# One core, a two-layer trunk in float32r: the SwiGLU's gate and up as seven block products for eight, the down projection in two passes

## The chip, the cores and the metric

The kernel runs on one core of a Trainium2 chip. The metric is device time in microseconds (us), from the first to the last instruction of the program with what lies around it; it is the median of three runs.

## The reference

The reference is a decoder trunk of two post-norm layers on 1024 tokens of 1024 features. Layer 0 mixes tokens by a convolution beside a spatial gate, layer 1 by an RWKV-7 recurrence. Behind each mixer stands a SwiGLU feed-forward with 2816 hidden channels, and it is these two feed-forwards that the change rewrites:

```python
D_MODEL, SEQ, DEPTH, FFN_HIDDEN = 1024, 1024, 2, 2816
ALPHA = (2.0 * DEPTH) ** 0.25

def swiglu_ffn(x, w_in, w_out):
    gate, up = jnp.split(x @ w_in, 2, axis=-1)
    return (jax.nn.silu(gate) * up) @ w_out

# every layer:  x <- LN(ALPHA * x + mixer(x));  x <- LN(ALPHA * x + swiglu_ffn(x))
```

## The kernel before

**Order of the program.** `phase_a` is the mixer of layer 0. `scan_const` builds the masks that the recurrence needs much later; it is some 85 operations on GpSimd. `ffn` follows for layer 0, then the projections and the scan of layer 1 (`phase_c`, `phase_d`), its output projection (`phase_e`), and `ffn` again. The order within each engine is made when the program is built: a scheduler places instructions by their dependencies, and each engine then runs its list in order.

**Dense products.** Each float32 operand is split into a head and a rest (`split`: ScalarE casts the head, VectorE subtracts it to get the rest; `load_unit` does this for a weight unit of 128x1024 at L185 and L186). A product is then three matmuls of 128x512 (head by head, head by rest, rest by head), written by `mm3` at L225 to L227.

**Norms ahead of the feed-forward.** `ln_to_T` norms a token tile of 128 tokens (`norm`, with a power on GpSimd at L265), transposes it on TensorE (`pt`, L284), applies gain and bias from PSUM into `lntmp` (VectorE and ScalarE in turn, L291 and L294), and splits it into eight pieces a layer half. `ln_rest` applies gain and bias to the token-major copy `acc` on GpSimd (L307, L308), one tile later; this copy is the residual.

**The feed-forward.** `up` makes one hidden tile of 128 channels: for each half of 512 tokens a gate product and an up product over eight feature tiles, so 2 x 2 x 8 x 3 = 96 matmuls, then silu, the product with the gate (`sg`, L578) and the split of the result (`hh`, `hl`). `down` takes hidden tiles in groups of two: for each token tile and each half of the output columns six matmuls into one PSUM bank, and VectorE adds the bank to `acc` (L595). The last group has four hidden tiles, and behind each token tile of it comes its final norm (`ln`, or `ln_out` for the output). There are 22 hidden tiles, so a feed-forward has 22 x 96 + 22 x 48 = 3168 matmuls. The first two hidden tiles begin with the first half of the tokens, while tiles of the second half are still being normed.

**Buffers.** Big tiles come from an arena of `N_ARENA` = 32 slots, raw loads from `N_RAW` = 3, weight units from `N_W` = 8, short-lived tiles from `N_T` = 6 and row broadcasts and masks (tag `row`) from 2.

Of the kernel before, what the change touches and what calls it, by code (L numbers as in the profile page):

```python
# [39 lines left out]
# columns: name -> number of [128] columns  # L40
# [44 lines left out]
def build(tc, xT, xtok, w_ab, w_abv, w_abo, cols, rows, hrows, sguw, f_in, f_out, w_r, w_k, w_v, w_o,  # L85
# [6 lines left out]
    with ExitStack() as es:  # L92
# [11 lines left out]
        xs, acc = phase_a(c, xT, xtok, w_ab, w_abv, w_abo, sguw, cols)  # L104
        show("a", acc)
        c.scan = scan_const(c)
        x1 = ffn(c, 0, xs, acc, f_in, f_out, "ffn0", fp32_out=True, spill=xres)
# [8 lines left out]
        xs, acc = phase_e(c, scry, xres, w_o, scan)  # L116
        if dbg is not None and "Y" in dbg:
            nc.sync.dma_start(dbg["Y"], scry)
        show("e", acc)
        ffn(c, 1, xs, acc, f_in, f_out, "ffn1", final=out)  # L120


# ---------------------------------------------------------------- helpers
# [52 lines left out]
def load_unit(c, src, arena=False, lo_eng=None):  # L176
    """A weight unit of [128, 1024]: raw load, then exact head / rest split."""
# [33 lines left out]
def act_half(c, name):  # L211
    """Split activations of 512 tokens, feature-major: 4 pieces of 2 feature tiles."""
# [8 lines left out]
def mm3(c, ps, lhs, rhs, start, stop, ls, rs):  # L221
    """ps += lhsT.T @ rhs with split operands; ls / rs slice them."""
# [7 lines left out]
def proj_T(c, ps, unit, xs, m=P):  # L230
    """ps[m, 512] = W[:, m columns].T @ x: feature-major output; unit is [128, 8 * m]."""
# [5 lines left out]
def proj_tok(c, ps, units, xs, t, turn=None):  # L237
    """ps[128 tokens, 512] = x.T @ W: token-major output; 4 units of [128, 2 * 512]."""
# [36 lines left out]
def ln_to_T(c, acc, tt, gname, g_row, b_row, dest, fp32_out=False, st=None, then=None):  # L275
    """LN of token tile acc (in place), and its transpose into dest (feature-major pieces)."""
# [3 lines left out]
    h, col = tt // 4, (tt % 4) * P  # L280
    for q in range(2):
# [3 lines left out]
        if not fp32_out:  # L285
            tm = tmp(c, "lntmp").rearrange("p (j t) -> p j t", j=4)
        for j in range(4):
            k = q * 4 + j
            d = dest[h][k // 2][:, k % 2, 1 + col:1 + col + P] if fp32_out else tm[:, j, :]
# [6 lines left out]
        if not fp32_out:  # L296
# [3 lines left out]
    c.rest = acc, g_row, b_row, then  # L300


def ln_rest(c):
    """Gain and bias of the token tile normed last: not needed soon, so behind the next one's norm."""
# [13 lines left out]
# ---------------------------------------------------------------- layer 0 mixer  # L318

def phase_a(c, xT, xtok, w_ab, w_abv, w_abo, sguw, cols):  # L320
# [15 lines left out]
    def load_consts():  # L336
# [6 lines left out]
        # keep s <= t: partition s, column t  # L343
# [7 lines left out]
    def pump(n=None):  # L351
        """A few steps of the convolution, to be done while the product traced last is."""
# [45 lines left out]
    def u_proj(j):  # L398
        """Feature tile j of the gated input, times the gate, and its split."""
# [15 lines left out]
    def v_proj(tt, units, v):  # L415
        """Token tile tt of the gate, up to its norm."""
# [118 lines left out]
    for tt in range(8):  # L535
# [9 lines left out]
        if tt % 4 == 3:  # L545
            xn[tt // 4] = act_half(c, "xm")
# [943 lines left out]
```

## Time and profile before

| what | value |
|---|---|
| runs of the kernel (us) | 2820.16, 2823.53, 2828.3; median 2823.53 |
| span of the profiled execution (us) | 2821.0 |
| TensorE busy, share of the span | 2686.7 us, 95% |
| VectorE busy | 1652.4 us, 59% |
| ScalarE busy | 1061.3 us, 38% |
| GpSimd busy | 753.0 us, 27% |
| mean granted TensorE clock | 0.974 |

The profile gives the span alone for the profiled execution; it stands 2.5 us under the median of the runs, and within their spread. PE is TensorE's matmuls, PEld its weight loads, DVE VectorE, ACT ScalarE, POOL GpSimd, SP the engine that issues most transfers. A row names line, engine, operation, and tiles as output<-inputs. `pu` and `pd` are the banks of the up and down products.

### The profile page before, as it was taken

Reading aid. Unit: us, or ns where it says so; the run is one execution under the profiler, and the core shown is the slowest. Engines: PE = TensorE matmul, PEld = TensorE weight load, DVE = VectorE, ACT = ScalarE, POOL = GpSimd, SP = SyncE. Lnnn points to the kernel's source line nnn. Section 1 sums busy time; section 2 is a strip of 40 time slices with the busy share of each in tenths; the row PEclk is TensorE's granted clock in tenths of the full one; section 3 lists DMA queues with packets and bytes.
Section 4 is the critical chain, followed back from the end, with each engine's and each line's share of the span. In section 5 each row is a group of like instructions: output and inputs, shape, how many; then the busy total and the mean of one; then the engine's idle time right before and its main releaser. Section 6 shows DMA issues by size and latency. Waiting matters only on the chain. (4 is left out here: it accounts for less than half of the span.)

```text
span 2821.0 us, 41373 instructions
## 1 busy us (share of the span) xinstructions
PE 2686.7 (95%) x16432; PEld 2180.9 (77%) x16432; DVE 1652.4 (59%) x2858; ACT 1061.3 (38%) x2060; POOL 753.0 (27%) x773
## 2 busy tenths in 40 slices
PE   8678999999999999799999999999989999999998
PEld 6466878888888887577777888888778888888887
DVE  7999673333333336878766899986663333333336
ACT  5435541111111113777655777775331111111111
POOL 4763472000000003210123777774340000000003
PEclk9889999999999999899998999999999999999999
DMA  4001302111111111445562222212211111111111
GB/s 162 30 15 46 112 31 74 45 45 48 57 45 45 47 51 49 153 135 183 153 212 96 71 83 67 68 54 91 101 53 53 45 45 57 48 45 45 53 45 60
DMA packets 119905, 205.98 MB, mean 73 GB/s; under 512 B 9888, under 2 KB 79648, under 8 KB 119712
## 3 DMA queue, kind: packets, MB, share of 16 engines
q1 hardware_dynamic: 117120, 196.01, 20.9%
q0 software_dynamic: 1440, 5.24, 0.5%
q8 instruction: 128, 2.10, 0.3%
q10 hardware_dynamic: 1152, 2.10, 0.2%
q14 instruction: 65, 0.53, 0.1%
HBM read 165.56 MB, written 37.75 MB: 72 GB/s over the span
## 5 line engine op out<-in xcount | busy, mean ns | idle before, releaser
L185 ACT CAST whi<-wraw 128x1024 fp32r<-128x1024 f32 x215 | 222.9, 1047 | 749.3 <-PE pd L226 355.7
L265 POOL TENSOR_TENSOR rstd<-ve,mhalf 128x1 f32<-128x1 f32 x48 | 40.6, 848 | 1470.3 <-DVE ve L263 1450.2
L186 DVE TENSOR_TENSOR wlo<-wraw,whi 128x1024 fp32r<-128x1024 f32 x215 | 271.5, 1271 | 244.5 <-ACT whi L185 216.5
L578 DVE TENSOR_TENSOR sg<-pu,sg 128x512 f32<-128x512 f32 x88 | 60.9, 692 | 500.8 <-PE pu L227 500.8
L595 DVE SCALAR_TENSOR_TENSOR acc<-acc,pd 128x512 f32<-128x512 f32 x320 | 218.2, 687 | 174.0 <-PE pd L227 173.9
L225 PE MATMUL pu<-xeh,whi 128*128 128x512 f32 x704 | 277.9, 395 | 0.0
L225 PE MATMUL pd<-whi,hh 128*128 128x512 f32 x704 | 277.3, 394 | 0.0
L227 PE MATMUL pd<-whi,hl 128*128 128x512 f32 x704 | 277.2, 394 | 0.0
L225 PE MATMUL pu<-xmh,whi 128*128 128x512 f32 x704 | 277.1, 394 | 0.0
L226 PE MATMUL pu<-xel,whi 128*128 128x512 f32 x704 | 276.8, 393 | 0.0
L226 PE MATMUL pu<-xml,whi 128*128 128x512 f32 x704 | 276.7, 393 | 0.0
L227 PE MATMUL pu<-xeh,wlo 128*128 128x512 f32 x704 | 276.7, 393 | 0.0
L226 PE MATMUL pd<-wlo,hh 128*128 128x512 f32 x704 | 276.7, 393 | 0.0
L227 PE MATMUL pu<-xmh,wlo 128*128 128x512 f32 x704 | 276.7, 393 | 0.0
L449 DVE SCALAR_TENSOR_TENSOR co<-yin,colt,co 128x512 f32<-128x512 f32 x150 | 167.3, 1126 | 1.7
L465 POOL TENSOR_TENSOR co<-ctap,co 128x512 f32<-128x512 f32 x90 | 144.1, 1602 | 51.0 <-ACT ctap L464 45.2
L227 PEld LDWEIGHTS pu<-xeh,wlo 128*128 128x128 f32 x704 | 132.3, 188 | 31.3
L226 PEld LDWEIGHTS pd<-wlo,hh 128*128 128x128 f32 x704 | 132.6, 188 | 30.7 <-DVE wlo L186 0.7
L225 PEld LDWEIGHTS pu<-xmh,whi 128*128 128x128 f32 x704 | 133.0, 189 | 30.0
L225 PEld LDWEIGHTS pu<-xeh,whi 128*128 128x128 f32 x704 | 132.7, 189 | 30.3
L226 PEld LDWEIGHTS pu<-xel,whi 128*128 128x128 f32 x704 | 132.5, 188 | 30.0
L225 PEld LDWEIGHTS pd<-whi,hh 128*128 128x128 f32 x704 | 133.0, 189 | 29.4
(300 smaller groups left out, 5796.8 us busy)
## 6 DMA issues: line engine op xcount, KB each, us to landing
wraw<-in_f_in_dram SPq DMA_DIRECT2D x88, 512.0 KB, 3.3
wraw<-in_f_out_dram SPq DMA_DIRECT2D x44, 512.0 KB, 3.2
wraw<-in_w_r_dram SPq DMA_DIRECT2D x16, 512.0 KB, 4.1
wraw<-in_w_k_dram SPq DMA_DIRECT2D x16, 512.0 KB, 3.8
wraw<-in_w_v_dram SPq DMA_DIRECT2D x16, 512.0 KB, 4.1
wraw<-in_w_ab_dram SPq DMA_DIRECT2D x12, 512.0 KB, 3.8
wraw<-in_w_o_dram SPq DMA_DIRECT2D x9, 512.0 KB, 4.1
xraw<-in_xT_dram SPq DMA_DIRECT2D x8, 512.0 KB, 10.4
```

What stands on the lines that cost most here:

```text
L185: nc.scalar.copy(hi, raw)
L186: (lo_eng or nc.vector).tensor_tensor(lo, raw, f(hi), op=ALU.subtract)
L225: nc.tensor.matmul(ps, ls(ah), rs(bh), start=start, stop=False)
L226: nc.tensor.matmul(ps, ls(ah), rs(bl), start=False, stop=False)
L227: c.last_mm = nc.tensor.matmul(ps, ls(al), rs(bh), start=False, stop=stop)
L265: c.last_pow = nc.gpsimd.tensor_tensor(r, ve, c.mhalf[:, 0:1], op=ALU.pow)
L449: pace(c, nc.vector.scalar_tensor_tensor(o, src(i), w(i), o, op0=ALU.mult, op1=ALU.add))
L465: nc.gpsimd.tensor_tensor(o, t_, o, op=ALU.add)
L578: nc.vector.tensor_tensor(sg, pp[1], sg, op=ALU.mult)
L595: nc.vector.scalar_tensor_tensor(an, an, ALPHA if first else 1.0, p, op0=ALU.mult, op1=ALU.add)
```

## The change

**Seven products for eight.** The weights of a hidden tile are a 2 x 2 block matrix A: the rows are gate and up, the columns the two halves of the features. The normed activations are a 2 x 2 block matrix B: the rows are halves of the features, the columns halves of the tokens. In place of the eight block products (of four feature tiles, 12 matmuls each) there are seven, of sums of blocks, and their results are added: 84 matmuls for 96. `Seven` holds the right-hand blocks. Two of them are blocks of B and are split as tiles are normed (`put` in `ln_to_T`). `combine` makes t1 and t2 on VectorE and t3 and t4 on GpSimd from pairs of token tiles (t, t + 4) and splits t1 to t4 and block 22: 40 splits of 128x2x128 a layer, all of them behind the norms of tiles 4 to 7. The left-hand sums s1 to s4 are made by VectorE for every hidden tile, and seven weight blocks are split (`block`). Banks px, py and pz hold running sums, so that results are added in PSUM where they share a prefix: VectorE reads py between one product and the next. `first` makes the two products that need no combination, for the first `JP` = 4 hidden tiles ahead of the rest.

**Down in two passes.** The hidden tile goes to DRAM (`scr_h`) and is loaded and split again in each pass. A pass makes 512 of the 1024 output columns: eight banks, one for each token tile, are summed over all 22 hidden tiles, and VectorE adds each to `acc` once a pass. The last `KEEP` = 6 hidden tiles stay split in the arena from pass 0 to pass 1; in pass 1 they run token tile by token tile (18 matmuls), each followed by its norm. The residual is stored to DRAM (`res`) behind `ln_rest` and loaded again at the start of pass 0.

**Buffers and queues.** The counts grow by one or two, row broadcasts are issued from SP's queue in place of GpSimd's, and the feed-forward's rows are loaded behind its up part.

```diff
-N_ARENA, N_W, N_RAW, N_T = 32, 8, 3, 6
+N_ARENA, N_W, N_RAW, N_T = 33, 9, 4, 8
...
-GF = 2            # hidden tiles of a group of the down projection
+JP = 4
+KEEP = 6
+BANKS = "bbbaaacc"
...
-    c.nc.gpsimd.dma_start(t[:, 0:n], row_ap[:, 0:n].to_broadcast([P, n]))
+    c.nc.sync.dma_start(t[:, 0:n], row_ap[:, 0:n].to_broadcast([P, n]))
...
-        if not fp32_out:
-            for e in range(2):
-                hi, lo = dest[h][q * 2 + e]
-                split(c, hi[:, :, col:col + P], lo[:, :, col:col + P], tm[:, 2 * e:2 * e + 2, :])
+        if not fp32_out and h == 0:
+            dest.put(c, ("11", "21")[q], tt, xt[:, q * 4:q * 4 + 4, :])
...
+class Seven:
...
+    def put(self, c, name, t, src):
...
+        s = slice(t % 4 * P, t % 4 * P + P)
+        for e, (hi, lo) in enumerate(self.B[name]):
+            split(c, hi[:, :, s], lo[:, :, s], src[:, 2 * e:2 * e + 2, :])
+
+    def combine(self, c):
+        nc = c.nc
+        new = lambda n: tmp(c, n).rearrange("p (k t) -> p k t", k=4)
+        for t in range(4):
+            (a1, a2), (b1, b2) = [(x[:, 0:4, :], x[:, 4:8, :]) for x in (self.x[t], self.x[4 + t])]
+            t1, t2, t3, t4 = new("t1"), new("t2"), new("t3"), new("t4")
+            nc.vector.tensor_tensor(t1, b1, a1, op=ALU.subtract)
+            nc.gpsimd.tensor_tensor(t3, b2, b1, op=ALU.subtract)
+            nc.vector.tensor_tensor(t2, b2, t1, op=ALU.subtract)
+            nc.gpsimd.tensor_tensor(t4, a2, t2, op=ALU.subtract)
+            self.put(c, "t2", t, t2)
...
+    def block(src):
...
+        split(c, hi, lo, src)
+        return hi, lo
+
+    def prod(ps, w, name, start=False):
+        for k in range(4):
+            (ah, al), (bh, bl) = w, xc.B[name][k // 2]
+            for i, (a_, b_) in enumerate(((ah, bh), (ah, bl), (al, bh))):
+                c.last_mm = nc.tensor.matmul(ps, a_[:, k * P:(k + 1) * P], b_[:, k % 2, :],
+                                             start=start and k == i == 0, stop=False, skip_group_check=True)
...
+    def first(j, raw):
...
+        prod(px, block(raw[:, 0:512]), "11", True)
+        nc.scalar.copy(p1, px)
+        yield
+        prod(px, block(raw[:, 512:1024]), "21")
+        nc.scalar.activation(sg, px, AF.Silu)
...
+    def hidden(j):
...
+        nc.vector.tensor_tensor(s1, a21, a22, op=ALU.add)
+        nc.vector.tensor_tensor(s2, s1, a11, op=ALU.subtract)
+        nc.vector.tensor_tensor(s3, a11, a21, op=ALU.subtract)
+        nc.vector.tensor_tensor(s4, a12, s2, op=ALU.subtract)
+        py, pz = bank(c, "b", "py"), bank(c, "c", "pz")
+        prod(py, block(s2), "t2", True)
...
+        if half is not None:
+            prod(pz, block(s1), "t1", True)
+            next(half)
+            p1 = done[j][0]
+            u2 = tmp(c, "u2")
+            nc.vector.tensor_tensor(u2, py, p1, op=ALU.add)
+            prod(py, block(s3), "t3")
+        p1, sg = done.pop(j)
+        hf = big(c, "hf")
+        nc.vector.tensor_tensor(u3, py, p1, op=ALU.add)
+        nc.vector.tensor_tensor(u3, pz, u3, op=ALU.add)
+        prod(py, block(a22), "t4")
...
+        prod(pz, block(s4), "22")
...
+        nc.sync.dma_start(hscr[j], hf)
...
+    def down(n):
+        s = slice(n * 512, (n + 1) * 512)
...
+            mm3(c, ps[tt], hs, w, i == 0, i == NHT - 1, lambda y: y[:, tt * P:(tt + 1) * P], lambda w_: w_)
+            if i == NHT - 1:
...
+                nc.vector.scalar_tensor_tensor(acc[tt][:, s], acc[tt][:, s], ALPHA, ps[tt], op0=ALU.mult, op1=ALU.add)
+                nc.vector.bn_stats(st[tt][:, n, :], acc[tt][:, s])
...
+        for i in range(NHT - KEEP if n else NHT):
+            hs, w = load(i)
...
+            for tt in range(8):
+                mm(tt, i, hs, w)
+        if n:
+            ops = [load(i) for i in tail]
+            for tt in range(8):
+                for i, (hs, w) in zip(tail, ops):
+                    mm(tt, i, hs, w)
...
+    for j in range(JP):
+        for _ in first(j, raw_load(c, f_in[layer, 2 * j])):
+            pass
+        if j == 0:
+            xc.combine(c)
+    for j in range(NHT):
+        hidden(j)
+    g_row, b_row = ln_rows(c, lnname)
+    down(0)
+    down(1)
```

**GpSimd's list at the masks, layer 0.** Before, the masks (`mtmp`, `mk64`, L938 to L949) end GpSimd's work until the final norms; the next entry is a power of those norms (`rstd`).

```order
L947 MEMSET mtmp_2844 128x64 [waits Pool_49]
L949 CAST mk64_0_2849<-mtmp_2844 128x256
L943 AFFINE_SELECT mtmp_2851<-mtmp_2851 128x128 [waits Pool_49]
L164 DMA g_row_2862<-in_rows_dram 128x1024 [waits Pool_49]
L945 AFFINE_SELECT mtmp_2851<-mtmp_2851 128x128 [waits Pool_49]
L947 MEMSET mtmp_2851 128x64 [waits Pool_49]
L949 CAST mk64_1_2856<-mtmp_2851 128x256
L164 DMA b_row_2864<-in_rows_dram 128x1024 [waits Pool_49]
L265 TENSOR_TENSOR rstd_6952<-ve_6950,mhalf_70 128x1 [waits DVE_49]
```

Now the last four sums of `combine` for token pairs 1, 2 and 3 stand at the end of the same masks (L1059 to L1070 are the same lines, renumbered; `xt` is a normed tile).

```order
L1068 MEMSET mtmp_2807 128x64 [waits Pool_49]
L1070 CAST mk64_0_2812<-mtmp_2807 128x256
L1064 AFFINE_SELECT mtmp_2814<-mtmp_2814 128x128 [waits Pool_49]
L334 TENSOR_TENSOR t4_2912<-xt_2282,t2_2910 128x512 [waits DVE_49]
L1066 AFFINE_SELECT mtmp_2814<-mtmp_2814 128x128 [waits Pool_49]
L1068 MEMSET mtmp_2814 128x64 [waits Pool_49]
L1070 CAST mk64_1_2819<-mtmp_2814 128x256
L332 TENSOR_TENSOR t3_2939<-xt_2650 128x512 [waits DVE_49]
L334 TENSOR_TENSOR t4_2940<-xt_2382,t2_2938 128x512 [waits DVE_49,Activation_49]
L332 TENSOR_TENSOR t3_2967<-xt_2684 128x512
L334 TENSOR_TENSOR t4_2968<-xt_2482,t2_2966 128x512 [waits DVE_49,Activation_49]
L267 TENSOR_TENSOR rstd_7405<-ve_7403,mhalf_70 128x1 [waits DVE_49]
```

Of the eight sums of `combine` in this layer three stand ahead of the masks, one ahead of the last three mask entries, and four behind all of them.

**VectorE's list behind them, layer 0.** These are the last rests of `combine` (`xcl`), the last two weight sums and the first rest of a weight sum, `wb_3113`, which the third matmul of the first py product reads. Before, VectorE had only rests of weights and of hidden results here.

```order
L198 TENSOR_TENSOR xcl_2880<-t1_2965,xch_2879 128x2x128 [waits Activation_49]
L198 TENSOR_TENSOR xcl_2886<-t3_2967,xch_2885 128x2x128 [waits Pool_49]
L198 TENSOR_TENSOR xcl_2870<-t2_2966,xch_2869 128x2x128 [waits Activation_49]
L198 TENSOR_TENSOR xcl_2872<-t2_2966,xch_2871 128x2x128 [waits Activation_49]
L198 TENSOR_TENSOR xcl_2888<-t3_2967,xch_2887 128x2x128
L198 TENSOR_TENSOR xcl_2902<-t4_2968,xch_2901 128x2x128 [waits Activation_49]
L198 TENSOR_TENSOR xcl_2904<-t4_2968,xch_2903 128x2x128 [waits Activation_49]
L646 TENSOR_TENSOR sums_3105<-wraw_3101,wraw_3103 128x512
L647 TENSOR_TENSOR sums_3106<-wraw_3101,sums_3106 128x512
L198 TENSOR_TENSOR wb_3113<-sums_3106,wb_3113 128x512
```

Ahead of these rows, from the entry that first waits for a buffer of the masks (`sums_3105<-wraw_3103`, with the wait Pool), stand 19 entries of this kind; from there to the last row here they are 28, of which 19 are rests of 128x2x128 and 9 are operations on 512 columns. VectorE's next ten entries are all on 512 columns, and the last of them is the sum `u2` that reads py. In layer 1 all 40 rests stand behind the last norm, and no mask stands among GpSimd's sums.

**TensorE's list in a hidden tile.** In the steady order py's third product is followed by four matmuls of the next tile's px, and then by py's fourth, which waits until VectorE has read py for u3. Before, one bank was read while two others were filled.

```order
L617 MATMUL py_3663<-xcl_2888,wb_3714 128x512
L617 MATMUL py_3663<-xch_2887,wb_3714 128x512 x2
L617 MATMUL py_3663<-xcl_2888,wb_3714 128x512
L617 MATMUL py_3663<-xch_2887,wb_3714 128x512
L617 MATMUL px_3774<-xch_2184,wb_3775 128x512
L617 MATMUL px_3774<-xcl_2185,wb_3775 128x512
L617 MATMUL px_3774<-xch_2184,wb_3775 128x512 x2
L617 MATMUL py_3663<-xch_2901,wb_3732 128x512 [waits DVE_49]
L617 MATMUL py_3663<-xcl_2902,wb_3732 128x512
L617 MATMUL py_3663<-xch_2901,wb_3732 128x512 x2
```

Of the 96 matmuls that `first` makes for four hidden tiles, 72 stand behind the transposes of token tile 7 in layer 0 and 74 in layer 1; the first py product stands behind them.

## Rows read from the trace of the kernel before

**Rows 1.** The page: busy time by engine; GB/s in 40 slices.

```profile
PE 2686.7 (95%) x16432; PEld 2180.9 (77%) x16432; DVE 1652.4 (59%) x2858; ACT 1061.3 (38%) x2060; POOL 753.0 (27%) x773
...
GB/s 162 30 15 46 112 31 74 45 45 48 57 45 45 47 51 49 153 135 183 153 212 96 71 83 67 68 54 91 101 53 53 45 45 57 48 45 45 53 45 60
```

**Rows 2.** Windows: busy us (and count) by engine, clock, DMA share, GB/s.

```profile
600.00:700.00 100.00, 100.00 (x436) 81.59 (x435) 37.95 (x50) 14.50 (x19) 0.00 (x0) 1.00 0.12 43
2500.00:2600.00 100.00, 100.00 (x436) 81.48 (x435) 38.98 (x51) 14.94 (x19) 0.00 (x0) 1.00 0.15 53
```

**Rows 3.** Groups by line: count, busy us, mean ns, idle before and releasers.

```profile
L186 DVE TENSOR_TENSOR wlo<-wraw,whi 128x1024 fp32r<-128x1024 f32 x215 | 271.5, 1271 | 244.5 <-ACT whi L185 216.5 <-PE pk L226 16.0 <-PE pl L226 2.2
L595 DVE SCALAR_TENSOR_TENSOR acc<-acc,pd 128x512 f32<-128x512 f32 x320 | 218.2, 687 | 174.0 <-PE pd L227 173.9
L196 DVE TENSOR_TENSOR hl<-sg,hh 128x512 fp32r<-128x512 f32 x88 | 61.0, 694 | 28.8 <-ACT hh L193 28.8
L308 POOL TENSOR_TENSOR acc<-acc,b_row 128x1024 f32<-128x1024 f32 x24 | 59.3, 2469 | 1.9
```

**Rows 4.** Timeline of TensorE around token tile 7, layer 0.

```profile
394.63 0.40 PE L227 MATMUL pu<-xmh,wlo 128*128 128x512 f32 x1
399.20 1.97 PE L284 MATMUL pt<-ident,acc 128*128 128x128 f32 x8 [4.17 <-ACT acc L272]
```

**Rows 5.** Timeline of GpSimd: the masks' first and last entries.

```profile
406.19 0.53 POOL L926 MEMSET mtmp<- 128x512 f32 x1
...
436.47 0.64 POOL L164 DMA_DIRECT2D g_row<-in_rows_dram  x1
...
437.58 1.19 POOL L949 CAST mk<-mtmp 128x256 uint8<-128x256 f32 x1
439.07 0.55 POOL L164 DMA_DIRECT2D b_row<-in_rows_dram  x1 [0.30 <-POOL mk L949]
```

**Rows 6.** Timelines of GpSimd and VectorE: norms of tiles 4 to 7, masks.

```profile
384.31 2.54 POOL L307 TENSOR_TENSOR acc<-acc,g_row 128x1024 f32<-128x1024 f32 x1
414.63 1.65 POOL L945 TENSOR_SCALAR_AFFINE_SELECT mtmp<-mtmp 128x128 f32<-128x128 f32 x1
...
385.20 4.46 DVE L196 TENSOR_TENSOR xml<-lntmp,xmh 128x256 fp32r<-128x256 f32 x2
389.90 0.41 DVE L196 TENSOR_TENSOR xml<-lntmp,xmh 128x256 fp32r<-128x256 f32 x1
415.69 0.69 DVE L196 TENSOR_TENSOR hl<-sg,hh 128x512 fp32r<-128x512 f32 x1 [0.69 <-ACT hh L193]
```

**Rows 7.** Groups by line on GpSimd and VectorE, 2760 to 2821 us.

```profile
L618 POOL TENSOR_TENSOR acc<-acc,g_row 128x512 f32<-128x512 f32 x7 | 9.1, 1299 | 7.9 <-ACT acc L617 7.9
L265 POOL TENSOR_TENSOR rstd<-ve,mhalf 128x1 f32<-128x1 f32 x8 | 7.9, 988 | 685.5 <-DVE ve L263 685.5
...
L621 DVE SCALAR_TENSOR_TENSOR acc<-acc,bmv,g_row 128x512 f32<-128x512 f32 x9 | 6.6, 741 | 0.0
```

**Rows 8.** Timeline of TensorE after an idle stretch, layer 1.

```profile
2079.34 0.78 PE L225 MATMUL pu<-xeh,whi 128*128 128x512 f32 x1
...
2081.89 0.39 PE L225 MATMUL pu<-xeh,whi 128*128 128x512 f32 x1
```

**Rows 9.** Timelines of TensorE and ScalarE at token tile 7, layer 1.

```profile
2088.63 1.09 PE L284 MATMUL pt<-ident,acc 128*128 128x128 f32 x8 [0.78 <-ACT acc L272]
2091.37 0.83 ACT L294 ACTIVATE lntmp<-pt,colt 128x128 f32<-128x128 f32 x2
```

**Rows 10.** Windows at the end of the first feed-forward.

```profile
1100.00:1120.00 20.00, 18.04 (x89) 14.17 (x88) 19.20 (x33) 11.55 (x20) 15.29 (x8) 1.00 0.13 53
```

**Rows 11.** Timeline of VectorE in the last norms: a token tile's period.

```profile
2785.24 0.69 DVE L595 SCALAR_TENSOR_TENSOR acc<-acc,pd 128x512 f32<-128x512 f32 x1 [0.44 <-PE pd L227]
2790.77 0.69 DVE L595 SCALAR_TENSOR_TENSOR acc<-acc,pd 128x512 f32<-128x512 f32 x1 [0.44 <-PE pd L227]
```

**Rows 12.** The page: weight loads, KB each, us from issue to landing.

```profile
wraw<-in_f_in_dram SPq DMA_DIRECT2D x88, 512.0 KB, 3.3
```

More of the change, by code (lines that the diff above doesn't have):

```diff
@@ L490, in conv_act, with ln @@
             split(c, hi[:, :, t * P:(t + 1) * P], lo[:, :, t * P:(t + 1) * P], ys[:, 2 * e:2 * e + 2, :])
-    xn = [None, None]
+    xc = Seven()
+    def ln(tt):
+        ln_to_T(c, acc[tt], tt, "mix0", rows_[0], rows_[1], xc,
+                then=lambda: nc.sync.dma_start(res[tt * P:(tt + 1) * P, :], acc[tt]))
     in_proj()
@@ L581, in ffn @@
-    dest = []
-    def down(js, hs, first, last):
-        units = [load_unit(c, f_out[layer, j]) for j in js]
-        for tt in range(8):
-            a = acc[tt]
-            if last:
-                st[tt] = norm_stats(c, D)
-            for n in range(2):
-                p = bank(c, "bc"[n], "pd")
-                for i in range(len(js)):
-                    mm3(c, p, hs[i], units[i], i == 0, i == len(js) - 1,
-                        lambda y: y[:, tt * P:(tt + 1) * P], lambda w: w[:, n * 512:(n + 1) * 512])
-                an = a[:, n * 512:(n + 1) * 512]
-                nc.vector.scalar_tensor_tensor(an, an, ALPHA if first else 1.0, p, op0=ALU.mult, op1=ALU.add)
-                if last:
-                    nc.vector.bn_stats(st[tt][:, n, :], an)
-            if last and final is not None:
-                ln_out(tt)
-            elif last and tt > 0:
-                ln(tt - 1)
-        if last and final is None:
-            ln(7)
-            ln_rest(c)
+    def block(src):
+        t_ = c.pool.tile([P, 1024], F32R, name="wb", tag="w", bufs=N_W)
+        hi, lo = t_[:, 0:512], t_[:, 512:1024]
+        split(c, hi, lo, src)
+        return hi, lo
@@ new lines, in hidden @@
+    def hidden(j):
+        raw, rup = raw_load(c, f_in[layer, 2 * j]), raw_load(c, f_in[layer, 2 * j + 1])
+        half = None
+        if j not in done:
+            half = first(j, raw)
+            next(half)
+        a11, a12, a21, a22 = raw[:, 0:512], raw[:, 512:1024], rup[:, 0:512], rup[:, 512:1024]
+        sums = [c.pool.tile([P, 1024], F32, name="sums", tag="row", bufs=2) for _ in range(2)]
+        s1, s3, s2, s4 = [t_[:, e * 512:(e + 1) * 512] for t_ in sums for e in range(2)]
+        nc.vector.tensor_tensor(s1, a21, a22, op=ALU.add)
[4 more added lines that the diff above has]
+        prod(py, block(s2), "t2", True)
+        if half is None:
+            p1 = done[j][0]
[3 more added lines that the diff above has]
+            prod(py, block(s3), "t3")
+        u3 = tmp(c, "u3")
+        if half is not None:
+            prod(pz, block(s1), "t1", True)
+            next(half)
+            p1 = done[j][0]
+            u2 = tmp(c, "u2")
+            nc.vector.tensor_tensor(u2, py, p1, op=ALU.add)
+            prod(py, block(s3), "t3")
+        p1, sg = done.pop(j)
[3 more added lines that the diff above has]
+        prod(py, block(a22), "t4")
+        up = tmp(c, "up")
+        nc.vector.tensor_tensor(up, py, p1, op=ALU.add)
+        nc.vector.tensor_tensor(hf[:, 0:512], up, sg, op=ALU.mult)
+        prod(pz, block(s4), "22")
+        nc.vector.tensor_tensor(u2, pz, u2, op=ALU.add)
+        nc.scalar.activation(u2, u2, AF.Silu)
+        nc.vector.tensor_tensor(hf[:, 512:1024], u3, u2, op=ALU.mult)
+        nc.sync.dma_start(hscr[j], hf)
@@ new lines, in ffn, with load_hidden, mm, load @@
+    acc, dest, kept = [None] * 8, [], {}
+    def load_hidden(i):
+        raw = raw_load(c, hscr[i])
+        hi, lo = big(c, "hh", F32R), big(c, "hl", F32R)
+        split(c, hi, lo, raw)
+        return hi, lo
+    def down(n):
+        s = slice(n * 512, (n + 1) * 512)
+        ps = [None] * 8
+        tail = list(range(NHT - KEEP, NHT))
+        def mm(tt, i, hs, w):
+            if i == 0:
+                ps[tt] = bank(c, BANKS[tt], "pd")
+            mm3(c, ps[tt], hs, w, i == 0, i == NHT - 1, lambda y: y[:, tt * P:(tt + 1) * P], lambda w_: w_)
+            if i == NHT - 1:
+                if n == 0:
+                    st[tt] = norm_stats(c, D)
+                nc.vector.scalar_tensor_tensor(acc[tt][:, s], acc[tt][:, s], ALPHA, ps[tt], op0=ALU.mult, op1=ALU.add)
+                nc.vector.bn_stats(st[tt][:, n, :], acc[tt][:, s])
+        def load(i):
+            hs = kept[i] if i in kept else load_hidden(i)
+            if n == 0 and i in tail:
+                kept[i] = hs
+            return hs, block(raw_load(c, f_out[layer, i][:, s], 512)[:, 0:512])
+        for i in range(NHT - KEEP if n else NHT):
+            hs, w = load(i)
+            if n == i == 0:
+                for tt in range(8):
+                    acc[tt] = big(c, "acc")
+                    nc.sync.dma_start(acc[tt], res[tt * P:(tt + 1) * P, :])
+            for tt in range(8):
+                mm(tt, i, hs, w)
+        if n:
+            ops = [load(i) for i in tail]
+            for tt in range(8):
+                for i, (hs, w) in zip(tail, ops):
+                    mm(tt, i, hs, w)
+                if final is not None:
+                    ln_out(tt)
+                elif tt > 1:
+                    ln(tt - 2)
+            if final is None:
+                ln(6)
+                ln(7)
+                ln_rest(c)
@@ L1413, in phase_e @@
     ln_rest(c)
-    return xn, acc
+    return xc
 def layout(i):
```

87 lines of the change are left out of this document (34 added, 53 removed).

## The prediction

> **What bounds the kernel now.** I read the page first: TensorE is busy 2686.7 of 2821.0 us, every other engine under 60% [rows 1]. Then windows inside the two feed-forwards: TensorE is full, 436 matmuls in 100 us at granted clock 1.00, or 0.2294 us each; VectorE is busy 38 to 39 us, ScalarE 15, GpSimd not at all [rows 2]. There a matmul left out is worth its whole 0.2294 us, and 60 us in 100 of VectorE lie free. Then the edges, where this cover is absent: the start of each feed-forward, where norms, splits and GpSimd's work decide, and its end. The change cuts the middle and loads both edges.
>
> **What is removed.** A hidden tile has 84 matmuls for 96, over 22 tiles and two layers 528 fewer; the down part keeps its number. 528 x 0.2294 = **-121.1 us**, if TensorE stays full.
>
> **The steady hidden tile.** 84 matmuls last 19.3 us. VectorE has 18 operations on 512 columns (four weight sums, seven rests, seven sums of results); a rest of that size takes 0.694 us [rows 3], so 12.5 us: it fits. The one tight place is py's fourth product, which waits for u3's read of py behind only four matmuls, 0.92 us. The read takes 0.69 [rows 3] and a hand-over on each side, so it is just covered; I charge 0.04 us a tile, 1.7 in all, if VectorE is free at that moment.
>
> **The down part.** Its operands cost VectorE 1.27 + 0.69 us for 24 matmuls, 5.5 us [rows 3]: hidden. Of the 320 additions to `acc`, 32 stay, which were hidden too [rows 2], so nothing is gained there. A pass's end and the turn from up to down I put at 1.5 us a layer, **+3.0**: eight additions of 0.69 us against a next step that needs the first bank at once; below nothing they can't be, and all eight unhidden on both turns would be 11 us a layer.
>
> **The start, layer 0.** This is the largest new cost. Before, TensorE waited 4.17 us for tile 7's norm, began its transposes at 399.20 and went on with up products [rows 4]. That norm stood behind splits of tiles 4 to 6 on VectorE, which now come later; I let the transposes end at about 397, with 72 matmuls of `first` behind them: 16.5 us of cover, to 413.5.
>
> The first py product needs all of t2 and a weight sum. VectorE's list reaches them behind an entry that waits for a buffer of the masks. The masks ran from 406.19 to 438.77, less 1.2 us for two transfers that GpSimd no longer issues: 31.4 us [rows 5]. They now begin at about 405 (the gain and bias of tile 7 some 4 us sooner, three sums of 1.30 us ahead) and end at 436. Behind them VectorE has 19 rests and 9 operations on 512 columns. A rest of 128x256 took 0.41 us when nothing was in its way and 4.46 for two when GpSimd's 128x1024 operations ran [rows 6]; so 19 x 0.41 + 9 x 0.69 = 14.0 us. In among them are GpSimd's last four sums, of 1.30 us (a 128x512 product there) [rows 7], each of which stops VectorE as the gain and bias did [rows 6]: 5.2. First py at 436 + 14.0 + 5.2 = 455.2, so TensorE waits **41.7 us**. Bounds: without the blocking 36.5; with the masks stretched by VectorE's work beside them, or less cover, 50.
>
> After an idle stretch the next six matmuls stood 0.43 us apart, 2.55 us in all, where 1.38 is normal [rows 8]: **+1.5** with a little for the longer wait. Then VectorE has no lead: `u2` of the first tile is its tenth operation after the split that released py, 6.9 + 0.7 us with its own time, against 24 matmuls, 5.5: 2.2 us late, and I charge the second tile as much: **+4.4**. From then on a tile of `first` has 60 matmuls, 13.8 us, against 16 operations, 11.0, and the lead grows.
>
> **The start, layer 1.** No masks. Tile 7 is normed 2.5 us after its transposes end [rows 9]; then come 38 rests and 8 operations, 21.1 us, GpSimd's four sums and one gain or bias of 2.4 us [rows 3], 7.6, and 1 for hand-overs: 32 us against 74 matmuls, 17.0. So 15 us of wait, 1.5 and 4.4 as above: **+21**. Bounds: 12 (no blocking) and 27 (two more gain and bias operations in the way).
>
> **The ends.** The first feed-forward hands over to work on VectorE, which is busy 19.2 of 20 us there [rows 10]; the last group gave it 5.5 us of matmuls a tile and now gives 4.1 for the same norm, with GpSimd's 4.9 us of gain and bias beside its power: **+4**. In the last norms a tile's period was 5.53 us, set by 24 matmuls [rows 11]; now 18 take 4.13. But GpSimd needs 1.30 + 1.29 + 0.99 and VectorE's two-input operations 2 x 0.74 [rows 7], which, taken as excluding each other, make 5.0: 0.8 us a tile longer than TensorE, seven tiles, **+6**.
>
> Here the trace bears on a rule. VectorE's rests, which read two tiles of SBUF, stand still for as long as GpSimd's gain and bias run [rows 6]. The Trainium skill, page "SBUF — State Buffer", section "Who interferes with whom", says that such a VectorE instruction and a GpSimd one that reads SBUF exclude each other for the whole instruction; by it, masks would also stop rests and be stopped, and the layer-0 wait would grow by some 6 us, an estimate from that page's rule. The trace shows a rest of 0.69 us that ran at full speed beside a mask of 1.65 [rows 6]; by it nothing is added, and the sum goes by that.
>
> **The sum.** -121.1 + 1.7 + 3.0 + (41.7 + 1.5 + 4.4) + 21 + 4 + 6 = -37.8 on the span of 2821.0: 2783.2, and with the 2.5 us by which the median of the runs stands above this span, **2785**. Layer 0 alone is near nothing: half of -121 is spent at its start. The case's own range is 2765 to 2806: the bounds above, not all on one side.
>
> **Rivals.**
> *The combination is cheaper than worked out.* Four raw buffers and nine weight units let loads and splits run ahead, VectorE's rests beside GpSimd are stopped less than before [rows 6], the turns cost nothing: the waits become 34 and 13 us, the ends +3. That is 7.7 + 8 + 7 + 5 = 28 less: 2757. For it: VectorE's additions from PSUM kept their 0.69 us beside GpSimd in the last norms [rows 11]. Against: the splits, which read SBUF twice [rows 6]. Chance 0.17.
>
> *py's fourth product waits in every tile.* If u3's read stands behind one other operation of 0.69 us on VectorE whenever it becomes ready, 44 tiles pay 0.69 each: +30, 2815. Two operations in front, 1.4 us: +61, 2846. It equals before at 38 / 44 = 0.86 us a tile and loses from there; that is the slower case. For it: four matmuls are the whole cover, and VectorE has 11 other operations a tile whose place is the scheduler's choice. Against: VectorE has 6.8 us free per tile. Chance 0.17: a third of it between one sixth and one operation (still faster), a third near one, a third beyond.
>
> *Transfers.* A pass loads 768 KB per hidden tile in 5.5 us, 143 GB/s, where the windows here show 43 to 53 [rows 2] and the page up to 212 in a slice [rows 1]; a weight load lands in 3.3 us [rows 12]. Were landing to take 2 us longer than the buffers bridge, 2 x 38 loads of hidden tiles would each cost 2 us: +150, 2935. Chance 0.02.
>
> *The clock.* A pass goes to another bank every three matmuls, where before a bank kept six. If TensorE stopped briefly at each, and the clock fell as it does after idle stretches, the 2112 matmuls of both layers' passes would run at 0.43 us: +420, 3205 [rows 8]. For it is only that row; against it, banks turn every six matmuls before, at clock 1.00 [rows 2]. In the Trainium skill, page "TensorE: Matmul & The Clock Gate", the section "A second HAM failure mode: psum-queue depth-cycling" tells of a kernel that lost throughput in this way by cycling through banks. Chance 0.02.
>
> **How the numbers follow.** The likeliest case has 0.62. A difference of 0.3%, 8.5 us, is about the least that a measurement of this kernel can tell from none: faster ends at 2815, slower begins at 2832. Faster: 0.62 + 0.17 + 0.05 = 0.84; same 0.06; slower 0.06 + 0.02 + 0.02 = 0.10. The range reaches down past the first rival's 2757 to 2745, and up past one operation in front of u3, to 2820; it leaves out the slower cases and little below.
>
> **What would show it.** In the profile after: a TensorE gap of 35 to 50 us near 413, ended by VectorE's `wb` rest, and one of 10 to 20 us near 2105; `t4`'s GpSimd rows behind the masks; windows in the up part with TensorE full, 84 matmuls per 19.3 us, and no idle before py's fourth product above 0.1 us; in the passes 436 matmuls in 100 us. A last-norm period near 5 us. I am wrong if py's fourth product shows idle of 0.7 us, if the gap at 413 is under 20, or if a pass shows waits on transfers.

## The result, and the profile after

The changed kernel takes 2778.95 us (median of 4 runs, 2777.77 to 2780.59), 0.984 of the kernel before (95% interval 0.9825 to 0.9856). The forecast was 2785, with a range of 2745 to 2820. The profiled execution has a span of 2778.9 us. One of the four runs of masks_start, below, stood in a slower state (3632 us at a granted clock of 0.637), and its time is the median of the other three.

The first rows to read are those that answer to [rows 1] and [rows 2]: the page's line of busy times, and windows of layer 0's start, of the up parts and of a pass of the down part (busy us and count of TensorE, its weight loads, VectorE, ScalarE and GpSimd; granted clock, DMA share, GB/s).

```profile
PE 2589.6 (93%) x15904; PEld 2089.1 (75%) x15904; DVE 1894.9 (68%) x3282; ACT 1225.9 (44%) x2404; POOL 769.9 (28%) x779
```

```profile
420.00:440.00 20.00, 0.00 (x0) 0.00 (x0) 3.93 (x6) 1.43 (x5) 19.19 (x60) 0.50 0.00 0
600.00:700.00 100.00, 100.00 (x431) 80.21 (x430) 62.08 (x93) 30.18 (x51) 0.00 (x0) 1.00 0.23 81
...
2200.00:2300.00 100.00, 100.00 (x433) 80.53 (x432) 61.89 (x93) 30.75 (x52) 0.00 (x0) 1.00 0.24 81
...
900.00:1000.00 100.00, 100.00 (x435) 81.59 (x434) 43.96 (x53) 32.31 (x41) 0.00 (x0) 1.00 0.49 163
```

TensorE has 528 matmuls less and is busy 97 us less, but its share of the span fell: there are 20 us in which it does nothing at all, while GpSimd is full. The up parts run at 431 to 433 matmuls in 100 us, the pass at 435, at clock 1.00.

The span between five marks that both kernels have shows where the 42 us came from. `pk` is layer 1's second projection, from which TensorE is full again.

| stretch | before | after | difference |
|---|---|---|---|
| start to the first up product | 379.2 | 376.1 | -3.1 |
| to the first `pk` (feed-forward 0, its end, the hand-over) | 835.7 | 831.3 | -4.3 |
| to the first up product of layer 1 | 856.9 | 862.5 | +5.5 |
| to the last `pd` (feed-forward 1) | 740.7 | 696.2 | -44.5 |
| to the end | 8.6 | 12.8 | +4.2 |

Both feed-forwards lost 264 matmuls, 60.6 us. Layer 1 kept most of it, layer 0 next to nothing. The +5.5 lie where neither kernel runs a feed-forward; the runs below, with the same code there, take 857.5 to 864.6, so much of this row may be the scatter of single profiles.

The chain of waits at layer 0's start says why layer 0 kept so little. First TensorE, where it waits ahead of transposes, where the first products stop in the middle and where the first py comes (compare [rows 4]):

```profile
385.58 2.82 PE L291 MATMUL pt<-ident,acc 128*128 128x128 f32 x12 [7.57 <-ACT xt L299]
...
409.33 0.40 PE L617 MATMUL px<-xch,wb 128*128 128x512 f32 x1
443.21 0.80 PE L617 MATMUL px<-xch,wb 128*128 128x512 f32 x1 [33.48 <-ACT p L628]
...
454.42 0.39 PE L617 MATMUL py<-xch,wb 128*128 128x512 f32 x1
```

Then ScalarE's timeline: the copy L628 stands behind casts for the combination, and the first of these waited for a sum on GpSimd.

```profile
436.83 0.71 ACT L195 CAST xch<-t 128x256 fp32r<-128x256 f32 x2 [21.73 <-POOL t L334]
439.28 1.94 ACT L195 CAST xch<-t 128x256 fp32r<-128x256 f32 x6 [1.75 <-POOL t L332]
441.96 0.71 ACT L195 CAST xch<-t 128x256 fp32r<-128x256 f32 x2 [0.74 <-POOL t L334]
442.57 1.06 ACT L628 COPY p<-px 128x512 f32<-128x512 f32 x2
```

Then GpSimd's and VectorE's (compare [rows 5]): the sum L334 stands among the last masks, and VectorE waits 18.43 us for a mask to give back a row buffer. The weight rest that the first py needs is the first of the three in the last row.

```profile
434.50 0.39 POOL L1070 CAST mk<-mtmp 128x256 uint8<-128x256 f32 x1
434.84 0.29 POOL L1064 TENSOR_SCALAR_AFFINE_SELECT mtmp<-mtmp 128x128 f32<-128x128 f32 x1
435.11 1.68 POOL L334 TENSOR_TENSOR t<-xt,t 128x512 f32<-128x512 f32 x1
```

```profile
413.60 2.89 DVE L198 TENSOR_TENSOR xcl<-xt,xch 128x256 fp32r<-128x256 f32 x6
434.92 0.75 DVE L644 TENSOR_TENSOR sums<-wraw 128x512 f32<-128x512 f32 x1 [18.43 <-POOL mk L1070]
...
452.62 1.89 DVE L198 TENSOR_TENSOR wb<-sums,wb 128x512 fp32r<-128x512 f32 x3
```

So the masks did hold VectorE, as forecast, but they also held ScalarE, and through it the first products that were to cover the wait.

### The profile page after: what moved, and what is told of

Read it like the earlier page. It is cut to its first block, busy times and chain, and to the rows that moved or that the text cites. A ratio compares the mean times of both kernels' runs of the same rounds, so it can differ in the third digit from the quotient of the medians.

```text
span 2778.9 us, 41747 instructions
## 1 busy us (share of the span) xinstructions
PE 2589.6 (93%) x15904; PEld 2089.1 (75%) x15904; DVE 1894.9 (68%) x3282; ACT 1225.9 (44%) x2404; POOL 769.9 (28%) x779
## 5 line engine op out<-in xcount | busy, mean ns | idle before, releaser
L617 PE MATMUL py<-xch,wb 128*128 128x512 f32 x1056 | 354.0, 397 | 4.6 <-DVE u L666 3.8
L198 DVE TENSOR_TENSOR wb<-wraw,wb 128x512 fp32r<-128x512 f32 x220 | 161.7, 739 | 182.0 <-ACT wb L195 181.2
L617 PE MATMUL px<-xch,wb 128*128 128x512 f32 x704 | 241.0, 406 | 41.8 <-ACT p L628 41.7
L229 PE MATMUL pd<-wb,hl 128*128 128x512 f32 x704 | 277.5, 394 | 0.0
L228 PE MATMUL pd<-wb,hh 128*128 128x512 f32 x704 | 277.0, 393 | 0.0
L227 PE MATMUL pd<-wb,hh 128*128 128x512 f32 x704 | 276.4, 393 | 0.0
L617 PEld LDWEIGHTS py<-xch,wb 128*128 128x128 f32 x1056 | 198.2, 188 | 62.9 <-DVE u L666 17.2
L617 PE MATMUL pz<-xch,wb 128*128 128x512 f32 x704 | 233.8, 393 | 0.0
L617 PE MATMUL py<-xcl,wb 128*128 128x512 f32 x528 | 207.3, 393 | 0.0
L188 DVE TENSOR_TENSOR wlo<-wraw,whi 128x1024 fp32r<-128x1024 f32 x83 | 112.2, 1355 | 73.5 <-ACT whi L187 29.1
L227 PEld LDWEIGHTS pd<-wb,hh 128*128 128x128 f32 x704 | 132.9, 189 | 30.0
L228 PEld LDWEIGHTS pd<-wb,hh 128*128 128x128 f32 x704 | 132.4, 188 | 30.3
```

Of the source, the lines that this page charges most:

```text
L188: (lo_eng or nc.vector).tensor_tensor(lo, raw, f(hi), op=ALU.subtract)
L198: return (eng or nc.vector).tensor_tensor(lo, src, f(hi), op=ALU.subtract)
L227: nc.tensor.matmul(ps, ls(ah), rs(bh), start=start, stop=False)
L228: nc.tensor.matmul(ps, ls(ah), rs(bl), start=False, stop=False)
L229: c.last_mm = nc.tensor.matmul(ps, ls(al), rs(bh), start=False, stop=stop)
L617: c.last_mm = nc.tensor.matmul(ps, a_[:, k * P:(k + 1) * P], b_[:, k % 2, :], start=start and k == i == 0, stop=False, skip_group_check=True)
```

## The experiments

**Theory.** The gain is matmuls left out; layer 0 loses it to the masks. Rivals: VectorE and GpSimd excluding each other decides both starts; VectorE's amount of work does; the down part gains or loses by itself. Spans between marks are from each run's profile, one execution each. Each time is a median; the kernel before, timed beside each group of runs, had medians of 2825.8 to 2827.9, so differences of 2 or 3 us between groups carry little. "Start" below is the time from the first up product to the first py, which is 78.3 us in layer 0 (376.1 to 454.4) and 42.6 in layer 1 (2069.9 to 2112.5) in the changed kernel.

**masks_early.**

```diff
+        c.scan = scan_const(c)
         xc = phase_a(c, xT, xtok, w_ab, w_abv, w_abo, sguw, cols, res[0])
-        c.scan = scan_const(c)
```

(The small table of `r_k` at the end of `scan_const` stays behind `phase_a`, since it reads columns that are loaded there.)

> The changed kernel with one edit: the scan's masks are built at the program's start, ahead of phase_a, where GpSimd lies idle until 25 us. Theory (masks hold layer 0's start: VectorE waits for one of their buffers, GpSimd's sums stand behind them, and ScalarE's copies of px behind those sums): the wait of 33.5 us on px at 409.7 falls to about the 8 us that layer 1 shows, the first py comes near 430 in place of 454.4, and the run takes 22 to 26 us less than the changed kernel, about 2755. Rival (VectorE and GpSimd excluding each other decides both starts, the masks only lie in that time): gain and bias and the sums exclude the rests as before, and under 8 us are gained.

Measured 2775.24 us, 0.9809 of before (0.9788 to 0.983): 4 us less than the changed kernel, which by the time alone would be the rival's. The trace says otherwise. Layer 0's start fell from 78.3 to 57.1 us, the 21 us near which the theory had it, but it began at 395.4 in place of 376.1. The loads of the kernel's first 45 us, on SP's queue, and TensorE there:

```profile
2.64 2.00 SPq L369 DMA_DIRECT2D xraw<-in_xT_dram  x3
30.07 0.33 SPq L167 DMA_DIRECT2D g_row<-in_rows_dram  x1
...
31.23 3.27 SPq L369 DMA_DIRECT2D xraw<-in_xT_dram  x4
...
39.38 0.80 PE L228 MATMUL pv<-xh,whi 128*128 128x512 f32 x1 [17.61 <-ACT xh L196]
```

The gain row's transfer, which the change moved from GpSimd's to SP's queue, now waited for a row buffer until the masks were done (GpSimd's last ends at 30.8), and every load behind it waited too: four `xraw` loads that the changed kernel issues from 4.72 on come from 31.23 on.

**masks_start.** The same move, and another kind of buffer for the masks:

```diff
-    mtmp = lambda n: c.pool.tile([P, 1024], F32, name="mtmp", tag="row", bufs=2)[:, 0:n]
+    mtmp = lambda n: tmp(c, "mtmp")[:, 0:n]
```

> The masks at the program's start as before, but in the short-lived tiles (tag t) and not in the two row buffers, for which the gain row's transfer waited until 30 us, with all loads of the first projection behind it on SP's queue. Theory (masks hold layer 0's start, worth 22 us, and the loss at the start came from the row buffers alone): the first px is back at 374 to 378, the stretch from there to the first pd product near 467 as in masks_early, in all 20 us below the changed kernel, about 2758. Rival (GpSimd's 27 us at the start hold the first projection in another way): the first px stays near 395, about 2775.

Measured 2762.40 us, 0.9773 (0.9754 to 0.9793): 16.5 less than the changed kernel; the first px is at 378.4, layer 0's start 57.2 us. The theory's two parts hold: the loss at the kernel's start is gone with the row buffers, and the gain of masks_early stays. The wait on px that is left is 13.0 us and still ends with the copy L628 (L629 there):

```profile
425.00 0.80 PE L618 MATMUL px<-xch,wb 128*128 128x512 f32 x1 [13.04 <-ACT p L629]
```

**sums_dve.**

```diff
-            nc.gpsimd.tensor_tensor(t3, b2, b1, op=ALU.subtract)
+            nc.vector.tensor_tensor(t3, b2, b1, op=ALU.subtract)
...
-            nc.gpsimd.tensor_tensor(t4, a2, t2, op=ALU.subtract)
+            nc.vector.tensor_tensor(t4, a2, t2, op=ALU.subtract)
```

> The changed kernel with t3 and t4 made by VectorE, the masks where they are. Theory: in layer 0 the weight sum still waits for a mask's buffer until about 435, but the rests no longer stand behind it, so the first py comes near 439, 15 us sooner; in layer 1 a sum of 1.3 to 3.4 us on GpSimd that stops VectorE becomes one of 0.69 on VectorE, 4 to 6 us sooner: about 2759. Rival (VectorE is the limit of the start, GpSimd's sums run beside it): eight more operations of 0.69 a layer cost 5 us each, about 2790.

Measured 2761.2 us, 0.9762 (0.9742 to 0.9782): 18 less, as the theory had it. Layer 0's start is 63.7 us, layer 1's 41.1, so 14.6 of it are in layer 0's start; the rival's cost of VectorE's extra work doesn't show. VectorE's wait for a mask's buffer is 4.38 us in place of 18.43. The first py still waited for the weight sum behind it:

```profile
434.31 0.75 DVE L644 TENSOR_TENSOR sums<-wraw 128x512 f32<-128x512 f32 x1 [4.38 <-POOL mk L1070]
...
437.45 0.79 PE L617 MATMUL py<-xch,wb 128*128 128x512 f32 x1 [6.82 <-ACT wb L195]
```

In layer 1 my 4 to 6 us were too much: 1.5 in the start.

**start_dve** is both edits, masks_start's and sums_dve's.

> Masks at the start in short-lived tiles, and t3 and t4 on VectorE. Theory (two waits in a row: the masks, then GpSimd's sums that stop VectorE and ScalarE's casts): both gains show, layer 0's stretch from first px to first pd falls from the 475 us of sums_dve to 460 to 463, about 2748. Rival (with either edit the rest of the start is the amount of VectorE's work): no more than 3 us below the better of masks_start and sums_dve.

Measured 2753.95 us, 0.974 (0.9725 to 0.9754): 7 below the better of the two. Layer 0's start is 51.6 us, 26.7 less than in the changed kernel. The two waits stood in a row, but the second edit adds 5.6 to masks_start's 21.1, no more. VectorE is now busy for 31.33 of the 31.40 us up to the first py (third pair of the row):

```profile
400.00:431.40 31.40, 23.59 (x80) 18.00 (x80) 31.33 (x63) 18.50 (x53) 6.73 (x3) 0.78 0.08 33
```

**start_late**, on top of start_dve.

```diff
-        if j == 0:
+        if j == JP - 1:
             xc.combine(c)
```

> As start_dve, and the combination written behind the first products of all four hidden tiles, so that ScalarE's copies of px stand ahead of its casts for the combination, and VectorE's first weight sums and rests ahead of most of its rests. Theory (TensorE's waits on px are ScalarE's copies behind casts that are not ready): the waits on px fall under 3 us in both layers; the first py comes some 5 us later, but VectorE then has 17 operations of 0.69 us in hand: 2 to 8 us below start_dve. Rival (VectorE's amount of work up to the first py decides, whoever stands first): the px waits turn into one of the same size ahead of py, within 2 us of start_dve or up to 6 above.

Measured 2758.43 us, 0.9759 (0.9743 to 0.9774): 4.5 above start_dve, with intervals that just overlap. The theory's gain did not come, and the time is the rival's. A row of the view of all waits (us in total, times, longest):

```profile
PE pz L618 <- ACT xch L196: 19.9, 2, 9.9
```

With the copies ahead, px no longer waits for the combination's casts; the first pz, placed ahead of the first py, waits 9.9 us a layer for the last of them instead. On VectorE some nine microseconds of weight work now stand ahead of the rests.

**mid1** is start_dve_ahead (below) with `if j == 1`, between the two.

> start_dve_ahead with the combination written behind the second hidden tile's first products, so that ScalarE's copy of the second px stands ahead of its casts, VectorE's list nearly as it was. Theory (the px waits of 2.9 and 6.9 us and VectorE's list end at nearly the same time, VectorE being busy without a break up to the rest that releases the first py): the px waits shrink, but py waits in their place, and at most 2 us are gained. Rival (TensorE waits for ScalarE's copies alone): 8 us less in layer 0 and 5 in layer 1.

Measured 2746.78 us, 0.9723 (0.9696 to 0.9751), against start_dve_ahead's 0.9731 (0.9717 to 0.9746): not told apart. In layer 0 the wait at px became 8.7 us in one place and 1.2 ahead of py, where it had been 2.9 and 6.9. The rival's 13 us are not there. VectorE's timeline in start_dve_ahead shows why: it is busy without a break, and the weight rest `wb` that the first py needs ends as TensorE comes to py at 428.59.

```profile
426.83 0.69 DVE L657 TENSOR_TENSOR sums<-wraw,sums 128x512 f32<-128x512 f32 x1
427.48 1.29 DVE L199 TENSOR_TENSOR wb<-sums,wb 128x512 fp32r<-128x512 f32 x2
```

So VectorE's work, and not the order of ScalarE's copies, sets the first py there.

**px_ahead.**

```diff
+        w4 = block(a22)
+        if JP <= j + 1 < NHT:
+            begun[j + 1] = begin(j + 1)
+        prod(py, w4, "t4", behind=True)
-        prod(py, block(a22), "t4")
```

`begin` loads the next tile's gate weights and issues its first px product; `behind` keeps the scheduler from placing py's fourth product ahead of it.

> The changed kernel with all 12 matmuls of the next tile's first px product, in place of 4, ahead of py's fourth product. Theory (py's fourth product waits some 0.15 us a tile for u3's read): 44 tiles give 5 to 7 us, about 2773. Rival (the loss of 0.3 us a tile against 84 matmuls at 0.2294 lies in every product, not at this wait): within 2 us of the changed kernel.

Measured 2775.43 us, 0.9809 (0.9788 to 0.9829), 3.5 less than the changed kernel: between the two, and within the scatter of the intervals. The trace shows how much is real. In the changed kernel py's fourth product opens with a step of 0.34 us between matmuls, 0.11 over the rest, in all 22 tiles of each layer:

```profile
605.25 0.50 PE L617 MATMUL py<-xch,wb 128*128 128x512 f32 x1
605.59 0.39 PE L617 MATMUL py<-xcl,wb 128*128 128x512 f32 x1
```

In px_ahead this step is gone from 18 of the 22, and the window of layer 0 has 434 matmuls in 100 us for 431:

```profile
620.00:720.00 100.00, 100.00 (x434) 81.16 (x433) 61.97 (x93) 30.34 (x51) 0.00 (x0) 1.00 0.25 85
```

From the first py to the first `pd` it takes 408.4 us for 410.9 in layer 0 and 409.0 for 410.0 in layer 1: 3.4 us in all. The wait is there, but 0.11 us a tile and not 0.15.

**start_dve_ahead** is start_dve with px_ahead's edit.

> As start_dve, with px_ahead's edit (12 matmuls ahead of py's fourth product). Theory (the two edits touch different stretches): 3 to 5 us below start_dve, about 2744. Rival (the start leaves VectorE with a backlog, so that the early px product only waits): within 1 us of start_dve.

Measured 2750.85 us, 0.9731 (0.9717 to 0.9746): 3.1 below start_dve, the theory's lower bound, though the intervals overlap.

**eight.** The up part makes gate and up by the plain products of four blocks of activations and four of weights; `combine`, `first` and the weight sums are out:

```diff
-            dest.put(c, ("11", "21")[q], tt, xt[:, q * 4:q * 4 + 4, :])
+            dest.put(c, (("11", "21"), ("12", "22"))[h][q], tt, xt[:, q * 4:q * 4 + 4, :])
...
+            prod(p, ws[j][2 * e], "1" + "12"[h], True)
+            prod(p, ws[j][2 * e + 1], "2" + "12"[h])
```

> The changed kernel with the eight plain block products in place of seven (no combination, no weight sums, 96 matmuls a hidden tile; hidden tiles to DRAM and the down part in two passes stay). It separates the two halves of the change. Theory (all of the gain is matmuls left out): the down part alone costs its turns and its two ends, some 12 us, so this one is near 2835, 0.3 to 0.6% above the kernel before. Rival (the down part gains by itself, with 32 additions from PSUM for 320 and more buffers): it is more than 8 us below the kernel before.

Measured 2829.51 us, 1.0011 of before (0.9995 to 1.0027): no difference that can be told. The down part in two passes, with its buffers, neither gains nor costs as a whole, and the seven products are worth the 50 us between this kernel and the changed one. The marks show costs and gains that cancel: 12.7 us more from the first up product to `pk`, 3.8 more behind the last `pd`, 7.8 less inside feed-forward 1, 3.4 less ahead of the first up product. The 12.7 lie behind layer 0's last `pd`, from which to `pk` it takes 91.5 us for 79.0; the changed kernel takes 91.6.

**keep7, keep8** are start_dve_ahead with `KEEP = 7` and `KEEP = 8`.

> start_dve_ahead with KEEP = 7: one more hidden tile in the last group of pass 1, so 21 matmuls (4.8 us) a token tile in place of 18 (4.13). Theory (behind the last groups the norms decide: 4.74 us a token tile by VectorE and GpSimd in turn in layer 1, VectorE full in layer 0): the last group begins 5.5 us sooner and its norms go on at their own pace, 4 to 5 us less in each layer, about 2742. Rival (the ends are set by TensorE, or by what follows the last product): within 2 us of start_dve_ahead.

> start_dve_ahead with KEEP = 8: 24 matmuls, 5.5 us a token tile. Theory: the last group begins 11 us sooner, but TensorE is now slower than the norms by 0.76 us over eight tiles, 6 us: in layer 1 some 5 us less than with KEEP = 6, the same as with 7; in layer 0, where VectorE needs more than 5.5 a tile, up to 9 less; about 2738 to 2742. Rival: within 2 us of start_dve_ahead, or above it if the two weight units that it holds longer starve the splits of the last group.

Measured 2737.56 us, 0.9684 (0.9662 to 0.9706), and 2741.73 us, 0.9696 (0.9675 to 0.9717): 13 and 9 below start_dve_ahead (keep8's interval touches that one's), and not told apart from each other. The reason is in the tails. In the changed kernel a token tile's last addition comes every 4.74 us and waits for nothing (compare [rows 11]); with seven it comes every 4.84, 21 matmuls, and waits for TensorE again.

```profile
2760.62 0.68 DVE L698 SCALAR_TENSOR_TENSOR acc<-acc,pd 128x512 f32<-128x512 f32 x1
2765.36 0.68 DVE L698 SCALAR_TENSOR_TENSOR acc<-acc,pd 128x512 f32<-128x512 f32 x1
```

```profile
2716.72 0.69 DVE L711 SCALAR_TENSOR_TENSOR acc<-acc,pd 128x512 f32<-128x512 f32 x1 [0.58 <-PE pd L230]
2721.56 0.69 DVE L711 SCALAR_TENSOR_TENSOR acc<-acc,pd 128x512 f32<-128x512 f32 x1 [0.68 <-PE pd L230]
```

From the last `pd` to the end keep7 takes 8.3 us for 12.3, and `pk` comes 5.1 sooner: the forecast 4 to 5 in each layer. A further 3.5 lie between `pk` and layer 1's first up product, where KEEP does nothing; they are within the scatter of that stretch. In keep8 the end takes 8.1 us too, and the stretch from the first px to `pk` 5.4 less than in start_dve_ahead.

**mid1_keep7.**

> All edits that gained, in one kernel: masks at the start in short-lived tiles, t3 and t4 on VectorE, the next px product ahead of py's fourth, the combination behind the second hidden tile's first products, KEEP = 7. Theory (the edits touch different stretches, so their gains add): 2737.6 less mid1's 3 to 5, about 2734, some 45 below the changed kernel. Rival (mid1's gain was the scatter between runs of one kernel): within 2 us of keep7.

Measured 2732.34 us, 0.9671 (0.9655 to 0.9687). It is the fastest here, 47 below the changed kernel and 93 below the kernel before; against keep7 the intervals overlap, so whether mid1 adds anything stays open.

## Why the prediction was right

The sign, the size and the place came out: 2779 for 2785, with almost all of the gain in layer 1. By its own steps:

- **528 matmuls less, -121.** The pace was read slightly too short: a window also counts the matmuls that only overlap its ends. From start to start a matmul took 0.2304 us in the first window of [rows 2] and 0.2308 in the changed kernel's pass (900 to 1000), so the pace held, and 528 are worth 121.7. At 0.2305, the 1752 matmuls behind the first py took 7.0 us too long in layer 0 (454.4 to 865.3) and 6.1 in layer 1. py's fourth product is 2.4 of this in each layer, forecast 0.9; the first tile's waits are 1.6 and 2.1, forecast 4.4; 0.95 is the last tile, which has no next px to cover its py. The cause of the other 2.0 and 0.7 no run here shows.
- **Layer 0's start, +43.2 (41.7 and 1.5).** The first py came at 454.4, forecast 455.2. The time of the first 96 up matmuls, to the start of the 97th, was 34.8 us before (379.2 to 414.0) and is 78.3 now: +43.4. The mechanism was half of it. VectorE's wait for the row buffer and the work behind it were as worked out (18.4 us from 434.92 to the end of the first py's rest, forecast 19.2), but the step that let TensorE finish the first products in the meantime failed. ScalarE's list was not looked at; its copies stood behind the casts, so the wait came at px, 409.7 to 443.2. It cost little only because VectorE was late as well: the rest that the first py needs ended at 453.3, 1.1 us ahead of it. That the sum agrees to 0.2 us is luck: at 0.2305 a matmul, 38.7 us were lost behind tile 7's transposes, 4.5 less than forecast, and 17.4 ahead of them, 5.5 more than before, which the forecast had not. There 24 up matmuls are left as cover for 42, and the wait of 7.57 us at 385.58 is new: tile 6's `xt` stood on VectorE behind seven weight rests of `first`, which took 8.62 us beside GpSimd's gain and bias.

```profile
374.45 8.62 DVE L198 TENSOR_TENSOR wb<-wraw,wb 128x512 fp32r<-128x512 f32 x7
```

- **GpSimd stops VectorE, 5.2.** The rests beside GpSimd's sums were stopped, and the sums too: they took 1.65 and 1.94 us each on average between 376 and 460 us in place of the 1.30 of [rows 7]. Beside the masks most rests kept their 0.41 us, but of the last eleven four took 0.62 to 1.00 (411 to 416 us). So the Trainium skill's rule (page "SBUF — State Buffer", section "Who interferes with whom") held for the sums, and for the masks only in part, where the forecast added nothing. That exclusion and the masks together are 26.7 of the 43.4 us (start_dve). The other 17 are in start_dve the wait of 7.57 us, still there, and behind it VectorE's own work, without a break; start_late and mid1, which only change the order, gain nothing there (57.2 and 52.5 us for 51.6).
- **Layer 1's start, +21.** Mis-sized. The 96 matmuls took 42.6 us for 32.1 before, +10.5, and 2.1 more came at the first reads of py: 12.6. Behind tile 7's transposes 12.9 us were lost where the forecast had 16.5; the first tile cost 2.1 for 4.4; and ahead of the transposes, which the forecast left out, 2.3 less was lost than before. The rests and sums stood as forecast, all 40 rests and four of the eight sums behind the transposes; but rests in a row start 0.34 us apart, where the sum has their 0.41 us of length, up to 2.7 us over 38. Here too the wait came at px (7.85 us, ended by L628).

```profile
2099.23 2.75 DVE L198 TENSOR_TENSOR xcl<-t,xch 128x256 fp32r<-128x256 f32 x8
```

- **Turns, +3.0.** Mis-sized: additions and first products of the next pass overlapped. All steps between `pd` products, both passes and the turn, were together 0.9 us over 0.2305 each in layer 0 (without the five that hold transposes) and 0.4 in layer 1.
- **The ends, +4 and +6.** The last norms ran at 4.74 us a tile, forecast 5.0, and the end came 4.2 us later, forecast 6. At layer 0's end the way from the last `pd` to `pk` grew by 12.6 us. TensorE is idle there for 18.9 us in place of 15.2, and within the last group for less than before; what the two come to against the forecast 4, the traces do not separate.
- **The whole.** 2779 for 2785 is closer than the terms: layer 1's start and the turns were put some 10 us too high, and the 5.5 us between the layers, which are no term of it, hide half of that.
- **The rivals.** py's fourth product waited a sixth of one operation (0.11 of 0.69 us), not one. No transfer ended a wait of TensorE in the up tiles or the passes. At banks that turn every three matmuls the clock stayed at 1.00, its 2.4 GHz level, over a whole pass at 435 matmuls per 100 us; what the Trainium skill tells of another kernel (page "TensorE: Matmul & The Clock Gate", section "A second HAM failure mode: psum-queue depth-cycling") does not show here.

## What to carry to other kernels

Fewer matmuls buy their full time where TensorE is full, and the preparation is paid where it is not: look for it at the edge, and read there the in-order list of every engine that TensorE touches, not only of the one that is full. A copy of half a microsecond behind casts that wait for another engine held TensorE for 33 us (here some 1 us of loss, since the next product's operands were late as well). Work that moves into an idle stretch takes its buffers along: building the masks early gained 21 us at one end and lost 19 at the other, until they had buffers that nobody on an in-order transfer queue waits for. Where a tail's norms and its matmuls are unequal, the number of matmuls in it can be chosen to match.

## What was not expected of the hardware

GpSimd's selects depend on the pattern: the masks of 128x128 with the finest blocks took 1.6 to 1.85 us each, with VectorE idle as well (1.61 in masks_early, at 3.81 us), the coarsest 0.29. After the idle 33.5 us TensorE's matmuls stood 0.43 us apart for some 4.8 us (443.2 to 448.0), as after the 5 us of [rows 8]; the granted clock was 0.50, the 1.2 GHz level, in the windows of 420 to 440 and of 444 to 447. So the stop of 33 us cost some 2.2 us on top of its own length (11 matmuls at 0.43 for 0.23). The one of 5 us cost 1.2 in its matmuls and 0.9 in the transposes between, which took 1.97 us for the 1.09 of [rows 9]: about the same.
